# The general path for tokens beyond an expert's slots: 64 unrolled copies become two nested loops on the chip

## The chip, the cores and the metric

The kernel runs on 1 core of one Trainium2 chip, as one launch. The metric is the device time in microseconds (us), the median over several executions. Less is better.

## The reference, cut to what matters

Two layers of a trunk on 256 tokens of width 1024. Each layer mixes tokens (projection, three branches, output projection), normalises, and then sends each token through 2 of 16 experts, chosen by a router whose weights both layers share:

```python
def moe(x2, w_router, router_bias, w1, w3, w2):
    expert_idx, gate_w = route(x2, w_router, router_bias)   # top-1 group of 4, top-2 inside it
    ...
    h = jax.nn.silu(xb @ w1[e]) * (xb @ w3[e])              # per expert: 1024 -> 512
    return h @ w2[e]                                        # 512 -> 1024
    ...
    return jnp.zeros((N + 1, D), x2.dtype).at[slot_tok].add(y)[:N]   # weighted by the gate
```

Everything is float32. An expert can be chosen by any number of tokens, so a kernel with a fixed number of places per expert needs a second path for the tokens that don't fit.

## The kernel before, in words

`body` (line 158) writes out both layers, one after the other, for five engines: TensorE (PE, with PEld for its weight loads), VectorE (DVE), ScalarE (ACT), GpSimd (POOL) and SyncE (SP). The order of each engine's instructions is the order in which the Python code makes them. That order is chosen while the program is built, by a small model of the engines' clocks (`Clock`, line 56): every operation made through the wrapper `Engine` (line 153, so nearly all rows carry L153) advances the model's clock of its engine, and waiting chains of work are put in where the model says that their inputs are ready. The model has no part in the execution.

The experts' part of a layer goes by seven units (`UNITS`, line 28, loop `for j in range(NU)` at line 1413). Six units hold two experts with 64 places each; unit 2 holds four experts with 32 places. The tokens of a unit are gathered into 128 columns (`xg`). For each unit PE does w1 (`hw`, 16 calls on a pair unit, 32 records), some combining of the unit before (`acc`), w3 (`hw` again), a transpose (`ht`) and w2 (`y`). A float32 product is two records per call, a transpose is one. Between these stand, in layer 0, products of the next layer's memory branch (`mk`, `mv`), and for the last two units the transposes that spread the norm's gain and shift (`ln`).

All weights come by DMA, issued on SP in one long stream (`plan` and `pump`; lines 215, 242, 252, 258 and 260 are its issues). A chunk goes into one of 27 slots of on-chip memory as soon as the slot is free, and an issue also waits for a transfer some places earlier to land. For a pair unit, w1, w3 and w2 are four chunks each, and each chunk is two issues (one for each expert), or four for the last. The last unit of a layer takes its w1 and w3 by line 242 and its w2 by lines 258 and 260, in layer 1 the last part of w2 by line 252. PE takes the chunks of w1 and w3 in the order in which they were issued, 8 records for each.

The router step counts the tokens of each expert. `fl` (line 1259) is 1 if a count is over 64 (32 for the four experts of unit 2), else 0. `Go` holds the gates of the tokens that found no place. After unit 5 (`j == NU - 2`, line 1522) `overflow(acc)` is called, once per layer. It is the general path: each engine loads `fl` into a register (line 1288, `TENSOR_LOAD` in the profile) and enters `tc.If(v_ > 0)` (line 1289, `COMPARE_BRANCH`). Inside, the tokens' vectors are transposed (`xo`, 8 times two transposes, 8 copies on DVE), and then all 16 experts times 4 quarters of the hidden width are computed for all 256 tokens, as 64 unrolled copies: 2 DMAs on POOL, 16 products, an activation on ACT, a multiply on DVE, two transposes of a gate column, a multiply on DVE, one more DMA on POOL, and 4 products that add to the accumulators `acc`. SP does nothing inside. Where the branch is not taken, each engine jumps over all that was written for it and then runs an `EVENT_SEMAPHORE` of line 1289 that waits until the engine's own earlier work is done and adds to its semaphore what the path inside would have added. What comes next on an engine stands behind that.

With these inputs the path inside is not taken: no record of `wt`, `xo`, `w2t` or of any other line inside the `If` is in the profile.

In PE's program the `If` stands between the last w2 product of unit 5 and the first w1 product of unit 6. In DVE's and ACT's it stands behind the first half of `scaled` for unit 5 (`yt<-y,gsl`), in SP's behind all issues of which the planner had slots: in layer 1 that is behind the last weight of the kernel.

Of the kernel before, what the change touches and what calls it, by code (L numbers as in the profile page):

```python
# [11 lines left out]
F32 = mybir.dt.float32  # L12
# [4 lines left out]
AF = mybir.ActivationFunctionType  # L17
OP = mybir.AluOpType
# [6 lines left out]
NE = 16  # L25
# [132 lines left out]
def body(tc, out, xT, xtok, memT, pos, cst, par, lay, pw, vb, lnr, wi, wik, wm, wb, wo, w1, w3, w2):  # L158
    nc = tc.nc
    ctx = ExitStack()  # L160
    clk = Clock()
    V, S, G, PE = (Engine(e, k, clk) for e, k in ((nc.vector, "V"), (nc.scalar, "A"), (nc.gpsimd, "G"), (nc.tensor, "P")))
# [4 lines left out]
    sm = ctx.enter_context(tc.tile_pool(name="sm", bufs=2))  # L167
# [8 lines left out]
    def tr(name):  # L176
        return clk.alloc("tr", 2, ps.tile([128, 512], F32, name=name, tag="tr", bufs=2))
# [25 lines left out]
    def again(slot, name, shape, dt=F32):  # L203
        return slots.tile(shape, dt, name=name, tag=held[slot])
# [23 lines left out]
    def get(*key):  # L228
        return live[key]
# [78 lines left out]
    ident = C[:, C_ID:C_ID + 128]  # L308
# [15 lines left out]
    def ln_col(l, w, k):  # L324
        o = P_LN + (l * 4 + w) * 8 + k
        return P[:, o:o + 1]
# [283 lines left out]
    key, shape, src = stream[0]  # L610
# [60 lines left out]
    for l in range(NL):  # L671
# [316 lines left out]
        if l == 0:  # L988
            for k in range(NL):
                o = P_BC + k * NB + B_G  # L990
# [152 lines left out]
        def rt(shape, name, dt=F32, tag=None):  # L1143
            return sm.tile(shape, dt, name=name, tag=tag or "r_" + name, bufs=1)
# [59 lines left out]
        Go = rt([128, 2, 16], "Go")  # L1204
# [82 lines left out]
        def overflow(acc):  # L1287
            v_ = nc.values_load(fl[0:1, 0:1], min_val=0, max_val=1)
            with tc.If(v_ > 0):
                xo = again("nh_h", "xo", [128, 8, 256])  # L1290
                for k in range(8):
                    p = tr("oxt")
                    for i in range(2):
                        PE.transpose(p[:, i * 128:(i + 1) * 128], xt[:, i, k * 128:(k + 1) * 128], ident)
                    if k < 4:
                        V.tensor_copy(xo[:, k], p[:, 0:256])
                    else:
                        V.tensor_scalar(xo[:, k], p[:, 0:256], ln_col(l, 0, k), ln_col(l, 1, k), op0=OP.mult, op1=OP.add)
                for e in range(NE):
                    for f in range(4):  # L1300
                        wt = again("nh_l", "wt", [128, 2, 8, 128])
                        fs = slice(f * 128, (f + 1) * 128)
                        for i, w in enumerate((w1, w3)):
                            nc.gpsimd.dma_start(wt[:, i], w[l, e].rearrange("p (k c) -> p k c", c=512)[:, :, fs])
                        ph = [tr("oh1"), tr("oh3")]
                        for w in range(2):
                            for k in range(8):
                                PE.matmul(ph[w][:, 0:256], wt[:, w, k], xo[:, k], start=k == 0, stop=k == 7)
                        w2t = again("nh_l", "w2t", [128, 1280])
                        ht = w2t[:, 1024:1280]  # L1310
                        S.activation(ht, ph[0][:, 0:256], AF.Silu)
                        V.tensor_tensor(ht, ht, ph[1][:, 0:256], op=OP.mult)
                        for i in range(2):
                            PE.transpose(ph[0][:, 256 + i * 128:384 + i * 128], Go[:, i, e:e + 1].broadcast_to([128, 128]), ident)
                        V.tensor_tensor(ht, ht, ph[0][:, 256:512], op=OP.mult)
                        nc.gpsimd.dma_start(w2t[:, 0:1024], w2[l, e, :, 1024 * f:1024 * f + 1024])
                        for i in range(2):
                            for hf in range(2):
                                PE.matmul(acc[i][hf], ht[:, i * 128:(i + 1) * 128], w2t[:, hf * 512:(hf + 1) * 512],
                                          start=False, stop=False)  # L1320


        acc = []
# [89 lines left out]
        for j in range(NU):  # L1413
# [20 lines left out]
            for nm in ("w1", "w3"):  # L1434
                early_mem(j, nm)
                p = tr("h" + nm)
                for q in range(4):
                    for kk in range(2):
                        k = 2 * q + kk
                        for a in range(len(ex)):  # L1440
                            o = jj * 128 + a * w_
# [50 lines left out]
            p = tr("ht")  # L1492
# [13 lines left out]
            if j < NU - 1:  # L1506
                yp = [pj("y"), pj("y")]
                for f in range(4):
                    for hf in range(2):
                        for a in range(len(ex)):  # L1510
                            PE.matmul(yp[hf][a * w_:(a + 1) * w_], hT[:, f, a * w_:(a + 1) * w_],
                                      get(l, "w2", j, f * len(ex) // 2 + a // 2)[:, a % 2, 0, hf * 512:(hf + 1) * 512],
                                      start=f == 0, stop=f == 3)
                    for b in range(len(ex) // 2):
                        if j == NU - 3 and f == 3:
                            done_as("xt", l, "w2", j, f)
                        else:
                            done(l, "w2", j, f * len(ex) // 2 + b)
                scaled(j, yt, yp[0], 0, 512)
                prev = (j, yp[1])  # L1520
                if j == NU - 2:
                    overflow(acc)
                    ring(NH if l + 1 == NL else RJ[2])
                    if l + 1 == NL:
                        held["gb"] = held.pop("nh_h")
                    else:
                        free("nh_h")
                    free("nh_l")
                if "gb" in held:
                    assert nxt[0] == len(stream)  # L1530
                    gb = load_gb(l, 2, again("gb", "gb", [128, 2, D]))
                continue

            pieces = [(0, 512), (512, 768)] + ([(768, 896), (896, 1024)] if tail else [(768, 1024)])
            for n, (lo_, hi_) in enumerate(pieces):
                p = (tr if n >= 2 else pj)("y")[:, 0:hi_ - lo_]
                for f in range(4):
                    q = f // 2 if n == 0 else min(n, 2) + 1
                    for a in range(2):
                        w = get(l, "w2", j, q)  # L1540
                        if n == 0:
                            w = w[:, 4 * a + 2 * (f % 2):4 * a + 2 * (f % 2) + 2].rearrange("p k c -> p (k c)")
                        elif hi_ - lo_ == 128:
                            w = w[:, 4 * (n - 2) + 2 * a + f // 2, 128 * (f % 2):128 * (f % 2) + 128]
                        else:
                            w = w[:, 4 * a + f]
# [197 lines left out]
```

## Time and profile before

| | us |
|---|---|
| median of 3 runs | 984.54 (983.82 to 985.46) |
| the profiled execution, its own time | 985.81 |
| its span, first to last instruction | 984.0 |
| PE busy | 928.5 (94% of the span) |
| DVE, ACT, POOL busy | 509.3, 372.8, 32.9 |
| data moved by DMA | 292.14 MB, mean 297 GB/s |
| TensorE clock granted, mean | 0.982 of full speed |

Times in the rows are microseconds from the span's start, in the timeline the start and the length of a group of instructions, its engine, line, operation, tiles and shapes, count, and in brackets the idle time before it and what ended that. A name ending in q (PEldq, DVEq) is an engine's sequencer: its register, branch and semaphore instructions, which don't count as busy time. [...]

### The profile page before, as it was taken

To read this page: it belongs to the slowest core of one execution; us is meant where nothing else is said; L and a number is where in the kernel's file an instruction comes from. 1 tells how busy PE (TensorE), PEld (TensorE's weight loads), DVE (VectorE), ACT (ScalarE), POOL (GpSimd) and SP (SyncE) were. 2 spreads that over 40 slices of the span, in tenths; PEclk is the share of its full clock that TensorE was granted. 3 is DMA by queue.
4 is the path that set the end of the run, shared out by engine and by line. 5 is a ranking of instruction groups with operands and counts; after the bars stand their busy time and mean duration, and the time that the engine had idled before them with its cause. 6 is when DMAs were issued, how large, how long until landed. Compare 5 with 4: busy or idle time off the path is not lost.

```text
span 984.0 us, 16526 instructions
## 1 busy us (share of the span) xinstructions
PE 928.5 (94%) x6450; PEld 681.3 (69%) x6450; DVE 509.3 (52%) x1042; ACT 372.8 (38%) x642; POOL 32.9 (3%) x29
## 2 busy tenths in 40 slices
PE   6999999989999999997998999999899899999974
PEld 6999999989954343433488999999899443434422
DVE  5879774559451111142388888854685412111226
ACT  5645667555241010121155644675552210101001
POOL 0000000000010000020022000000000000000101
PEclk9999999999999999998999999999999999999988
DMA  9933263309999999999995213265199999999994
GB/s 345 424 147 125 87 257 129 130 23 417 420 420 365 419 418 419 420 419 417 412 394 197 104 47 118 98 270 201 59 419 420 326 369 419 419 419 419 418 410 138
DMA packets 74461, 292.14 MB, mean 297 GB/s; under 512 B 7168, under 2 KB 13312, under 8 KB 64128
## 3 DMA queue, kind: packets, MB, share of 16 engines
q1 hardware_dynamic: 74368, 290.94, 74.5%
q8 instruction: 54, 0.88, 0.3%
q14 instruction: 39, 0.32, 0.1%
HBM read 289.86 MB, written 1.05 MB: 296 GB/s over the span
## 4 chain that ended last, share of the span: by engine, by line
PE 34%; issue 30%; DMA 26%; DVE 3%; POOL 2%; ACT 1%; SPq 0%; POOLq 0%; DVEq 0%; another core or an unknown queue 0%
DMA ck_w<-w 26%; PE g L153 7%; PE hw L153 5%; PE wb L153 4%; PE wo L153 2%; PE y L153 2%; PE gx L153 2%; PE mv L153 1%; POOL xt L153 1%; PE q L153 1%; PE k L153 1%; PE mq L153 1%; PE u L153 1%; PE v L153 1%; DVE xt L153 1%
## 5 line engine op out<-in xcount | busy, mean ns | idle before, releaser
L153 PE MATMUL hw<-ck_w,xg 128*64 128x512 f32 (+1 forms) x1024 | 218.3, 609 | 15.1 <-DMA ck_w<-w 8.6
L153 PEld LDWEIGHTS hw<-ck_w,xg 128*64 128x64 f32 (+1 forms) x1024 | 66.0, 132 | 146.8 <-issue 111.5
L153 PE MATMUL g<-x_h,wsp 128*128 128x256 f32 x768 | 146.6, 287 | 0.0
L153 PEld LDWEIGHTS g<-x_h,wsp 128*128 128x128 f32 x768 | 121.8, 191 | 1.5 <-issue 0.7
L153 PE MATMUL g<-x_l,wsp 128*128 128x256 f32 x384 | 108.6, 283 | 0.0
L153 DVE SCALAR_TENSOR_TENSOR yt<-y,gsl,yt 128x512 fp32r<-128x512 f32 (+1 forms) x29 | 21.0, 723 | 160.4 <-ACT yt L153 160.4
L153 PE MATMUL y<-ck_w,hs 128*64 128x512 f32 (+3 forms) x560 | 101.1, 559 | 1.1 <-ACT hs L153 0.9
L153 DVE TENSOR_TENSOR wsp<-ck_g,wsp 128x1024 fp32r<-128x1024 f32 x48 | 58.7, 1224 | 43.8 <-ACT wsp L153 43.5
L153 PEld LDWEIGHTS y<-ck_w,hs 128*64 128x64 f32 (+1 forms) x560 | 34.1, 130 | 58.7 <-issue 49.0
L153 PEld LDWEIGHTS g<-x_l,wsp 128*128 128x128 f32 x384 | 73.6, 192 | 0.2
L153 ACT ACTIVATE yt<-y,gsl 128x512 fp32r<-128x512 f32 (+2 forms) x31 | 20.0, 646 | 97.0 <-PE y L153 93.6
L153 ACT CAST wsp<-ck_g 128x1024 fp32r<-128x1024 f32 x48 | 50.0, 1042 | 0.0
L153 PE MATMUL wo<-wsp,mg 128*128 128x256 f32 x384 | 49.2, 285 | 0.0
L153 ACT COPY hs<-ht 128x256 f32<-128x256 f32 x14 | 5.2, 373 | 112.0 <-PE ht L153 112.0
L153 PEld LDWEIGHTS wo<-wsp,mg 128*128 128x128 f32 x384 | 46.9, 192 | 0.0
L153 ACT ACTIVATE hs<-hw 128x512 f32<-128x512 f32 x14 | 8.4, 599 | 94.9 <-PE hw L153 94.9
L153 DVE TENSOR_TENSOR hs<-hs,hw 128x512 f32<-128x512 f32 x14 | 9.6, 688 | 64.7 <-PE hw L153 64.7
L153 DVE TENSOR_TENSOR wsp<-ck_wb,wsp 128x1024 fp32r<-128x1024 f32 x24 | 29.4, 1223 | 19.8 <-ACT wsp L153 19.8
L153 ACT ACTIVATE g<-g,P 128x256 f32<-128x256 f32 x48 | 22.7, 473 | 41.0 <-PE g L153 40.7
L153 PE MATMUL iq<-x_h,wsp 128*128 128x256 f32 x128 | 28.7, 322 | 7.5 <-ACT wsp L153 7.5
L153 ACT CAST wsp<-ck_wb 128x1024 fp32r<-128x1024 f32 x24 | 25.1, 1045 | 22.1 <-PE wb L153 21.6
L153 ACT ACTIVATE xg<-gx,P 128x256 f32<-128x256 f32 (+1 forms) x40 | 20.8, 522 | 25.7 <-PE gx L153 25.3
(281 smaller groups left out, 1795.0 us busy)
## 6 DMA issues: line engine op xcount, KB each, us to landing
ck_w<-w SPq DMA_DIRECT2D x286, 512.0 KB, 10.0
ck_w<-w SPq DMA_DIRECT2D x48, 1024.0 KB, 17.7
ck_g<-wi SPq DMA_DIRECT2D x24, 1024.0 KB, 4.9
ck_wb<-wb SPq DMA_DIRECT2D x12, 1024.0 KB, 4.8
ck_wo<-wo SPq DMA_DIRECT2D x8, 1024.0 KB, 6.1
ck_mk<-wm SPq DMA_DIRECT2D x4, 1024.0 KB, 10.5
ck_mv<-wm SPq DMA_DIRECT2D x4, 1024.0 KB, 11.4
ck_q<-wi SPq DMA_DIRECT2D x4, 1024.0 KB, 16.6
```

The source lines that it names most:

```text
L153: return f(*args, **kw)
```

## The change

The two Python loops over experts and quarters inside the `If` become two nested loops on the chip (`tc.For_i`). What is inside is written once. The slices of the weights are addressed by the loop registers, and the gate column is first copied to a small tile `ge`, from which the transposes read. The `If`, its condition and its place stay, and nothing outside it is touched.

```diff
-                for e in range(NE):
-                    for f in range(4):
-                        wt = again("nh_l", "wt", [128, 2, 8, 128])
-                        fs = slice(f * 128, (f + 1) * 128)
-                        for i, w in enumerate((w1, w3)):
-                            nc.gpsimd.dma_start(wt[:, i], w[l, e].rearrange("p (k c) -> p k c", c=512)[:, :, fs])
...
-                        V.tensor_tensor(ht, ht, ph[1][:, 0:256], op=OP.mult)
-                        for i in range(2):
-                            PE.transpose(ph[0][:, 256 + i * 128:384 + i * 128], Go[:, i, e:e + 1].broadcast_to([128, 128]), ident)
-                        V.tensor_tensor(ht, ht, ph[0][:, 256:512], op=OP.mult)
-                        nc.gpsimd.dma_start(w2t[:, 0:1024], w2[l, e, :, 1024 * f:1024 * f + 1024])
...
+                with tc.For_i(0, NE) as e, tc.For_i(0, 4) as f:
+                    wt = again("nh_l", "wt", [128, 2, 8, 128])
+                    for i, w in enumerate((w1, w3)):
+                        src = w[l].rearrange("e p (k f c) -> e p k f c", f=4, c=128)[bass.ds(e, 1), :, :, bass.ds(f, 1)]
+                        nc.gpsimd.dma_start(wt[:, i], src.rearrange("e p k f c -> p (e k) (f c)"))
...
+                    V.tensor_tensor(ht, ht, ph[1][:, 0:256], op=OP.mult)
+                    ge = sm.tile([128, 2], F32, name="ge", tag="ve")
+                    V.tensor_copy(ge, Go[:, :, bass.ds(e, 1)].rearrange("p i o -> p (i o)"))
+                    for i in range(2):
+                        PE.transpose(ph[0][:, 256 + i * 128:384 + i * 128], ge[:, i:i + 1].broadcast_to([128, 128]), ident)
+                    V.tensor_tensor(ht, ht, ph[0][:, 256:512], op=OP.mult)
+                    src = w2[l].rearrange("e p (f c) -> e p f c", f=4)[bass.ds(e, 1), :, bass.ds(f, 1)]
+                    nc.gpsimd.dma_start(w2t[:, 0:1024], src.rearrange("e p f c -> p (e f c)"))
```

The lines left out are the same on both sides but for their indentation: the two products with `xo`, the activation, and the four products into `acc`.

## Rows read from the trace of the kernel before

**Rows 1.** The page: busy us and instructions; then busy tenths of DMA in 40 slices.

```profile
PE 928.5 (94%) x6450; PEld 681.3 (69%) x6450; DVE 509.3 (52%) x1042; ACT 372.8 (38%) x642; POOL 32.9 (3%) x29
...
DMA  9933263309999999999995213265199999999994
```

**Rows 2.** Instructions of line 1289, both layers: duration ns min/median/max, first and last start.

```profile
L1289 PEldq COMPARE_BRANCH  x2: 5808/5880/5952, 453.5 to 933.8; - x2
L1289 ACTq COMPARE_BRANCH  x2: 45/45/45, 457.1 to 934.9; - x2
L1289 DVEq COMPARE_BRANCH  x2: 68/70/72, 458.0 to 935.7; - x2
L1289 PEldq EVENT_SEMAPHORE  x2: 51/51/51, 459.4 to 939.9; - x2
L1289 ACTq EVENT_SEMAPHORE  x2: 17/17/17, 462.1 to 935.4; - x2
L1289 SPq COMPARE_BRANCH  x2: 45/49/53, 462.2 to 962.0; - x2
L1289 DVEq EVENT_SEMAPHORE  x2: 21/21/21, 463.4 to 941.1; - x2
```

**Rows 3.** Timeline of PE behind the branch of layer 0, and the last w2 part.

```profile
463.67 5.00 PE L153 MATMUL hw<-ck_w,xg 128*64 128x512 f32 x16 [6.33 <-DMA ck_w<-w]
...
493.39 1.95 PE L153 MATMUL y<-ck_w,hs 128*64 128x256 f32 x16
```

**Rows 4.** Timeline of PE in layer 1: first, last w3 chunk, end.

```profile
941.36 8.52 PE L153 MATMUL hw<-ck_w,xg 128*64 128x512 f32 x32 [6.03 <-DVEq L1289]
...
957.55 1.94 PE L153 MATMUL hw<-ck_w,xg 128*64 128x512 f32 x8
...
970.67 1.25 PE L153 MATMUL cb<-yt,Pq 128*128 128x128 f32 x8
```

**Rows 5.** Timeline of DVE: its last operation ahead of each branch.

```profile
457.32 0.75 DVE L153 SCALAR_TENSOR_TENSOR yt<-y,gsl,yt 128x512 fp32r<-128x512 f32 x1 [5.68 <-ACT yt L153]
...
935.28 0.75 DVE L153 SCALAR_TENSOR_TENSOR yt<-y,gsl,yt 128x512 fp32r<-128x512 f32 x1 [6.37 <-ACT yt L153]
```

**Rows 6.** Instruction fetches: the page's DMA kinds, whole span (packets, MB, share).

```profile
q8 instruction: 54, 0.88, 0.3%
```

**Rows 7.** DMA kinds in the stretch 933 to 946 us, around layer 1's branch.

```profile
q8 instruction: 2, 0.03, 0.9%
q14 instruction: 3, 0.02, 0.4%
```

**Rows 8.** Windows: us, busy times (instructions) of PE, PEld, DVE, ACT, POOL, PEclk, DMA share, GB/s.

```profile
463.70:470.20 6.50, 6.50 (x29) 3.09 (x30) 2.23 (x2) 0.45 (x1) 0.00 (x0) 0.79 1.03 416
935.30:941.40 6.10, 0.07 (x3) 0.07 (x3) 0.73 (x1) 0.00 (x0) 0.00 (x0) 0.68 1.03 413
941.40:947.90 6.50, 6.50 (x24) 2.29 (x26) 0.00 (x0) 0.00 (x0) 0.00 (x0) 0.78 1.03 415
820.00:900.00 80.00, 79.36 (x469) 32.78 (x466) 13.25 (x28) 11.00 (x19) 0.00 (x0) 1.00 1.03 419
```

**Rows 9.** Issues of w1's first chunk in layer 0, unit 6 (line 242).

```profile
L242 SPq DMA_DIRECT2D ck_w<-w x2: 338/338/338, 443.3 to 444.4; - x2
...
DMA to landing us min/median/max: 11.8/11.8/11.8
```

**Rows 10.** The last issue of w2 in layer 0 (line 260).

```profile
L260 SPq DMA_DIRECT2D ck_w<-w x1: 1130/1130/1130, 476.0 to 476.0; - x1
...
DMA to landing us min/median/max: 8.7/8.7/8.7
```

**Rows 11.** The last issue of w3 in layer 1 (line 242).

```profile
L242 SPq DMA_DIRECT2D ck_w<-w x1: 674/674/674, 943.7 to 943.7; - x1
...
DMA to landing us min/median/max: 10.8/10.8/10.8
```

**Rows 12.** Issues of w2's first two chunks in layer 1 (line 258), behind the branch's fetches.

```profile
DMA to landing us min/median/max: 9.8/9.9/10.0
```

More of the change, by code (lines that the diff above doesn't have):

```diff
@@ L1298, in overflow @@
                         V.tensor_scalar(xo[:, k], p[:, 0:256], ln_col(l, 0, k), ln_col(l, 1, k), op0=OP.mult, op1=OP.add)
-                for e in range(NE):
-                    for f in range(4):
-                        wt = again("nh_l", "wt", [128, 2, 8, 128])
-                        fs = slice(f * 128, (f + 1) * 128)
-                        for i, w in enumerate((w1, w3)):
-                            nc.gpsimd.dma_start(wt[:, i], w[l, e].rearrange("p (k c) -> p k c", c=512)[:, :, fs])
[L1305 to L1311, printed above, removed]
-                        V.tensor_tensor(ht, ht, ph[1][:, 0:256], op=OP.mult)
-                        for i in range(2):
-                            PE.transpose(ph[0][:, 256 + i * 128:384 + i * 128], Go[:, i, e:e + 1].broadcast_to([128, 128]), ident)
-                        V.tensor_tensor(ht, ht, ph[0][:, 256:512], op=OP.mult)
-                        nc.gpsimd.dma_start(w2t[:, 0:1024], w2[l, e, :, 1024 * f:1024 * f + 1024])
[L1317 to L1320, printed above, removed]
@@ new lines, in overflow @@
+                with tc.For_i(0, NE) as e, tc.For_i(0, 4) as f:
[3 more added lines that the diff above has]
+                        nc.gpsimd.dma_start(wt[:, i], src.rearrange("e p k f c -> p (e k) (f c)"))
+                    ph = [tr("oh1"), tr("oh3")]
+                    for w in range(2):
+                        for k in range(8):
+                            PE.matmul(ph[w][:, 0:256], wt[:, w, k], xo[:, k], start=k == 0, stop=k == 7)
+                    w2t = again("nh_l", "w2t", [128, 1280])
+                    ht = w2t[:, 1024:1280]
+                    S.activation(ht, ph[0][:, 0:256], AF.Silu)
+                    V.tensor_tensor(ht, ht, ph[1][:, 0:256], op=OP.mult)
[6 more added lines that the diff above has]
+                    nc.gpsimd.dma_start(w2t[:, 0:1024], src.rearrange("e p f c -> p (e f c)"))
+                    for i in range(2):
+                        for hf in range(2):
+                            PE.matmul(acc[i][hf], ht[:, i * 128:(i + 1) * 128], w2t[:, hf * 512:(hf + 1) * 512],
+                                      start=False, stop=False)
```

## The prediction, made before the change was run

> **What bounds the kernel now.** I first read the page's slices: the DMA engines are full from the tenth slice to the twenty-first and again from the thirtieth to the last but one, stretches that take in the experts' stages of both layers [rows 1]. There the weights set the pace. Then I looked for the changed lines. Nothing inside the `If` left a record, so with these inputs the path is skipped in both layers, and all the change can move is what it costs to skip it. The view of line 1289 shows that cost [rows 2]. PE's branch takes 5.81 and 5.95 us by itself, at 453.5 and 933.8. DVE's takes 0.07, but its next instruction comes 5.4 us after it both times (458.0 to 463.4, 935.7 to 941.1). ACT loses 5 us in layer 0 (457.1 to 462.1), nothing in layer 1 (934.9 to 935.4). SP, with nothing inside, passes in 0.05.
>
> PE's timeline shows what comes of it: idle 6.33 and then 6.03 us [rows 3, 4]. PE starts again 0.27 us after DVE's late instruction both times (463.4 to 463.67; 941.1 to 941.36), and in layer 1 the trace names it. In layer 0 it names a DMA. I don't follow it there: the first product behind the branch needs the first chunk of w1, issued at 443.3 and 444.4 and landed 11.8 us later, by 456.2 [rows 9]. So PE waits for DVE, and DVE for its own jump.
>
> What is in the jump? The skipped code of DVE is 8 copies and 64 times 2 operations, 136 and the waits. That of PE is 16 transposes, and 64 times 16 + 4 products and 2 transposes. At four instructions for a product (two records, each with a weight load) and two for a transpose that is 32 + 64 x 84, some 5,400. The trace's fetches say how far that is: PE and PEld executed 12,900 instructions [rows 1] in a run with 54 packets on queue 8 [rows 6], 239 for each, so PE jumps over some 22 packets' worth. And around the branch of layer 1 the fetch queues moved two packets for PE and three for the others in 13 us [rows 7], where 54 in 984 us would be 0.7 for PE. I read the 5 to 6 us as waiting for code that had not been fetched, behind a full DMA system.
>
> **The change part by part.** *Copies removed.* Inside are left 8 + 3 operations on DVE, one on ACT, and on PE 32 + 84 = 116 instructions, with the loops' own control some 150: 0.6 of a packet. The skip then ends in code that is being fetched ahead anyway. That a short skip is free is shown by ACT in layer 1 (64 activations, 0.4 us) and by SP. That ACT's same skip cost 5 us in layer 0 says that it depends on where the code lies, and bounds the claim: per branch the cost is between 0.05 and 5.95 us. I take 0.2, since the skip is now much shorter than ACT's.
>
> [...]
>
> *Layer 0.* DVE's last operation ends at 457.32 + 0.75 = 458.07 [rows 5]; with 0.2 for the branch and 0.27 for the handover PE starts at 458.5 instead of 463.67: 5.2 us. Then the clock: PE runs at 0.79 of full speed for 6.5 us behind the stall [rows 8], 1.4 us of work lost, which an idle of about 1 us should not bring about (bounds 0 and 1.4). So 5.2 to 6.6. Do the weights allow it? The last issue of w2 lands at 476.0 + 8.7 = 484.7 [rows 10], and PE uses it at 493.39 [rows 3]: room for 8.7. The earlier chunks have as much or more, so it isn't taken back there. What is late next is PE itself, and behind it the start of layer 1, which takes its input from these products; there DMA is half idle [rows 1], so the shift is handed on until the weights of layer 1 start, that many us earlier. I take 6.5.
>
> *Layer 1.* PE could start at 935.28 + 0.75 + 0.47 = 936.5, 4.9 earlier, with the same 1.4 of clock. But here PE has little to gain on: the last of w3 lands at 943.7 + 10.8 = 954.5 [rows 11], and PE begins those products at 957.55 [rows 4]. 3.05 us is all, unless the weights come earlier. They might: issues land after 10.8 us here, and after 9.9 just behind [rows 12], so the fetches may hold the stream up by 0.9; by the moved bytes (413 and 415 against 419 GB/s [rows 8]) it is 0.15. So 3.2 to 4.0; I take 3.5. The weights are late next.
>
> *Added work.* The copy to `ge`, the address arithmetic and the loops' control are inside and not run: 0, whatever they cost. *Left as it is:* the five loads of the flag. *Order.* The planner's clock now goes through the body once instead of 64 times. What it decides afterwards depends on differences between engines; after one pass as after 64, PE is last and ACT first, so I expect the same order: 0, with 1.5 us either way if some chain moves. POOL's skip is long done when POOL is next needed: 0, and SP's costs 0.05 now.
>
> **Sum.** 6.5 + 3.5 = 10.0. The profiled execution took 985.81 in all (span 984.0 and 1.8 around it), so it would take 975.8; it lies 1.27 above the median of 984.54, which makes 974.5. With the bounds 8.4 and 10.6, and 1.5 for the order: 972.4 to 977.6.
>
> **The rivals.**
>
> *Half of it.* One jump in one layer still misses, or the DMA that the trace names in layer 0 was the true end of that wait. Then one term is left: 984.5 - 6.5 = 978.0, or 984.5 - 3.5 = 981.0. For it: ACT, with one miss and one hit on the same code. Against: 11 DVE operations are a twelfth of 136.
>
> *The distance isn't it.* DVE's 5.4 us would be something that every taken branch of DVE has here, and PE's 5.9 would hide behind it. Then nothing moves: 984.5. For it: DVE skips only 136 operations, far less than PE, and yet waits as long. Against: ACT's 0.4 us in layer 1, and the three packets on queue 14 in [rows 7]. [...]
>
> [...]
>
> **How the numbers follow.** Both stalls go: 0.62. Half: 0.13. No change: 0.08. Barrier: 0.17. The likeliest is 974.5. A measurement of this kernel can tell about 0.2%, 2 us. The range leaves out the barrier and reaches over the half case to the no-change case, and down by the 1.5 of the order and some 2 us for the layer border, where DVE and POOL share a stretch that may fall together differently: 970.5 to 984.5. Faster is the first two and a little of the third: 0.76; same 0.07; slower 0.17.
>
> **What would show it.** Right: line 1289 on PE and DVE under 0.5 us, PE idle about 1 us at either branch, the granted clock full behind it, the weights' DMA full as before, and layer 1 starting some 6 us earlier. In layer 1 PE should now wait for single chunks of w3. Wrong: DVE's next instruction still 5 us behind its branch; PE waiting on another engine's line 1289 until SP arrives; new semaphore or drain instructions on the way around; or layer 0 gaining and the start of layer 1 not.

## The result, and the profile after

The changed kernel takes 979.27 us, median of 4 runs (978.02 to 979.70), beside 984.99 us for the kernel before (4 runs, 983.82 to 985.46; one more than stood in its table). The ratio is 0.9935 [0.9916, 0.9954] (in brackets the 95% interval): faster by 5.7 us, 0.6%, where the forecast of 974.5 said 10. The profiled execution took 979.70, its span is 978.0; both are 6.0 to 6.1 under those of the kernel before.

The page of the changed kernel comes first: busy us and instructions of PE, then the busy tenths of DMA in 40 slices and the instruction fetches (packets, MB, share).

```profile
PE 927.9 (95%) x6450; PEld 680.7 (70%) x6450; DVE 510.2 (52%) x1042; ACT 372.7 (38%) x642; POOL 32.7 (3%) x29
...
DMA  9943263309999999999996213266199999999995
...
q8 instruction: 52, 0.85, 0.3%
q14 instruction: 31, 0.25, 0.1%
```

Each engine executes as many operations as before [rows 1]. Two fetch packets fewer arrive on queue 8 (54 before, [rows 6]). The full stretches of DMA stand where they stood. (By these rows a packet of queue 8 is 16 KB and one of queue 14 is 8 KB. That PE's code comes on queue 8 and DVE's and ACT's on queue 14 is inferred from the packets' times, in the table under runs 4, 9 and 12.)

The view of line 1289 of the changed kernel answers to [rows 2].

```profile
L1289 PEldq COMPARE_BRANCH  x2: 318/336/353, 454.1 to 931.5; - x2
L1289 ACTq COMPARE_BRANCH  x2: 45/48/50, 457.8 to 932.9; - x2
L1289 ACTq EVENT_SEMAPHORE  x2: 17/17/17, 457.9 to 933.0; - x2
...
L1289 DVEq COMPARE_BRANCH  x2: 56/64/72, 458.6 to 933.3; - x2
L1289 DVEq EVENT_SEMAPHORE  x2: 21/21/21, 458.8 to 933.7; - x2
L1289 SPq COMPARE_BRANCH  x2: 45/49/53, 462.8 to 958.6; - x2
```

PE's branch costs 0.3 us instead of 5.9. DVE's event comes 0.2 to 0.4 us behind its branch instead of 5.4. ACT loses nothing in either layer (0.2 us). SP still comes last and nobody waits for it. POOL's jump, for which nobody waits, ends 0.2 to 0.5 us behind its branch instead of 5.1. So the jumps are cheap on every engine, and no barrier took their place: PE restarts at 459.07 and 934.00, SP passes at 462.8 and 958.6.

What PE made of it is in its timeline (only groups behind an idle time, and the three that answer to [rows 3, 4]), with its waits at the layer border in the kernel before below.

```profile
459.07 3.65 PE L153 MATMUL hw<-ck_w,xg 128*64 128x512 f32 x16 [1.12 <-DVEq L1289]
...
487.45 1.95 PE L153 MATMUL y<-ck_w,hs 128*64 128x256 f32 x16
...
524.54 0.45 PE L153 MATMUL ikw<-x_h,wsp 128*72 128x256 f32 x2 [3.21 <-DVE wsp L153]
531.19 0.39 PE L153 MATMUL q<-x_h,wsp 128*128 128x256 f32 x1 [2.31 <-ACT iqs L153]
...
934.00 6.88 PE L153 MATMUL hw<-ck_w,xg 128*64 128x512 f32 x26 [1.01 <-DVEq L1289]
...
951.02 1.95 PE L153 MATMUL hw<-ck_w,xg 128*64 128x512 f32 x8
...
964.66 1.25 PE L153 MATMUL cb<-yt,Pq 128*128 128x128 f32 x8
```

```profile
517.48 0.39 PE L153 MATMUL iq<-x_l,wsp 128*128 128x256 f32 x1 [0.42 <-DVE x_l L153]
...
520.25 0.39 PE L153 MATMUL iq<-x_l,wsp 128*128 128x256 f32 x1 [1.79 <-DVE x_l L153]
...
535.11 0.39 PE L153 MATMUL q<-x_h,wsp 128*128 128x256 f32 x1 [1.05 <-ACT iqs L153]
```

Read as a walk along the program, each start against its partner before:

| place | before | after | ahead of before |
|---|---|---|---|
| PE's branch, layer 0 [rows 2] | 453.5 | 454.1 | -0.6 |
| last w2 part, layer 0 [rows 3] | 493.39 | 487.45 | 5.94 |
| PE's branch, layer 1 [rows 2] | 933.8 | 931.5 | 2.3 |
| last w3 chunk, layer 1 [rows 4] | 957.55 | 951.02 | 6.53 |
| last products [rows 4] | 970.67 | 964.66 | 6.01 |

Layer 0 gained 0.6 + 5.94 = 6.5 us, layer 1 gained 6.01 - 2.3 = 3.7. These are the two terms of the forecast, 6.5 and 3.5. The 0.6 us by which the changed kernel was behind came near 400 us, ahead of the first branch; between the traces of the runs below this difference goes from 2.0 behind to 1.9 ahead, so I don't count it as the change's.

But of the 5.94 us only 2.3 were left at the second branch. I matched the two traces product by product (PE executes them in the same order but for one exchanged pair near 875 us) and call the time by which a product starts earlier the lead. It is still 5.93 in `iq` of layer 1 (516 us before), grows to 10.15 near the end of `iq`, is 3.92 when `q` begins and 2.42 some 2.5 us later; then it stays between 2.1 and 2.7 up to layer 1's branch. So 3.3 us were lost within 30 us, at the layer border, where PE now waits for `wsp` (a chunk of weights, split in two parts for the products) and `iqs` (524.54 and 531.19 above).

The windows of the changed kernel show the clock (us, busy times of PE, PEld, DVE, ACT, POOL, PEclk, DMA share, GB/s; PEclk is the mean of the TensorE clock granted, 1.00 at full speed, DMA share the busy share of the 16 DMA engines).

```profile
458.00:464.00 6.00, 4.93 (x27) 2.61 (x28) 3.05 (x3) 1.99 (x2) 0.00 (x0) 1.00 1.03 417
...
524.00:530.00 6.00, 4.34 (x22) 4.09 (x22) 5.79 (x12) 0.42 (x1) 0.00 (x0) 0.72 0.53 178
530.00:536.00 6.00, 4.81 (x27) 4.81 (x28) 3.69 (x5) 5.59 (x8) 0.00 (x0) 0.72 0.98 374
...
936.00:942.00 6.00, 5.71 (x23) 1.88 (x22) 0.00 (x0) 0.00 (x0) 0.00 (x0) 1.00 1.03 417
```

At the border of the kernel before:

```profile
518.00:524.00 6.00, 4.21 (x24) 4.01 (x24) 6.00 (x3) 1.19 (x3) 4.36 (x2) 0.75 0.45 150
```

Behind both branches the granted clock is now full, where it was 0.79 and 0.78 [rows 8]. At the border it fell in the kernel before too, in this one stretch (0.96 in the next, full behind that); now it is 0.72 in two, with the waits for `wsp` and `iqs`.

What held `wsp` is in DVE's timeline of the changed kernel, with POOL's beside it: four operations of one gain-and-shift step (`next_x`, `xt<-xt,gb`).

```profile
511.19 10.64 POOL L153 TENSOR_TENSOR xt<-xt,gb 128x1024 f32<-128x1024 f32 x4 [15.15 <-DMA gb<-lnr]
...
512.11 2.50 DVE L153 CAST aux<-aux 128x256 f32<-128x256 int32 x1
514.64 2.46 DVE L153 TENSOR_SCALAR aux<-aux,rc 128x256 f32<-128x256 f32 x1
517.13 4.85 DVE L153 TENSOR_SCALAR aux<-aux 128x256 f32<-128x256 f32 x2
```

In the kernel before the same stretch reads so:

```profile
511.64 10.79 POOL L153 TENSOR_TENSOR xt<-xt,gb 128x1024 f32<-128x1024 f32 x4 [9.67 <-PE xtr L153]
...
512.25 2.35 DVE L153 TENSOR_TENSOR x_l<-xraw,x_h 128x512 fp32r<-128x512 f32 x1
514.53 0.53 DVE L153 TENSOR_SCALAR xraw<-xtr,P 128x256 f32<-128x256 f32 x1
514.99 5.21 DVE L153 TENSOR_TENSOR x_l<-xraw,x_h 128x512 fp32r<-128x512 f32 x2
520.12 4.53 DVE L153 TENSOR_TENSOR wsp<-ck_iq,wsp 128x1024 fp32r<-128x1024 f32 x2
524.57 0.28 DVE L153 CAST aux<-aux 128x256 f32<-128x256 int32 x1
524.89 0.35 DVE L153 TENSOR_SCALAR aux<-aux,rc 128x256 f32<-128x256 f32 x1
```

This is the main reading. POOL's stretch stayed at 511 to 522 us, because it now starts when the row `gb` (gain and shift) has landed: issued at 495.3, that transfer takes 15.7 us behind a full weight stream (DMA share 1.00 to 1.01 from 495 to 511 us), and POOL waits 15.15 us for it. Before, the row was issued at 494.7 and landed after 16.8 us, at 511.5, as the transposes `xtr` ended for which POOL waited there. All the rest moved 6 us ahead beneath it. Before, POOL's four operations stood beside four of DVE: three on `x_l` and the first of the two splits of `iq` (3.40 us; the second, behind POOL's end, takes the usual 1.23). Now they stand beside four operations on `aux` (the rotary angles, called rope below), each of which takes 2.4 to 2.5 us instead of 0.28 to 0.35. The split of `ikw`, for which PE waits, comes behind them. The second wait comes through ACT: its `iqs<-iq` at 530.68 stands behind its two operations on `aux` (529.24 and 530.36), and these wait for the rope (9.58 and 0.70 us). The operations hit before are short again (`x_l` 0.69 to 0.74 us, the split 1.23), which is the growth to 10.15; the loss behind it is larger.

In layer 1 the weights capped the gain as forecast. The changed kernel's last issue of w3 (line 242, answering to [rows 11]):

```profile
L242 SPq DMA_DIRECT2D ck_w<-w x1: 333/333/333, 941.0 to 941.0; - x1
...
DMA to landing us min/median/max: 10.0/10.0/10.0
```

It lands at 951.0 and PE begins on it at 951.02. The 3.05 us of room that it had before are used up to the last tenth.

### The profile page after: what moved, and what is told of

Same layout as the page of the kernel before. It is cut to its first block, busy times and chain, and to the rows that moved or that the text cites. A ratio compares the mean times of both kernels' runs of the same rounds, so it can differ in the third digit from the quotient of the medians.

```text
span 978.0 us, 16510 instructions
## 1 busy us (share of the span) xinstructions
PE 927.9 (95%) x6450; PEld 680.7 (70%) x6450; DVE 510.2 (52%) x1042; ACT 372.7 (38%) x642; POOL 32.7 (3%) x29
## 3 DMA queue, kind: packets, MB, share of 16 engines
HBM read 289.86 MB, written 1.05 MB: 297 GB/s over the span
## 4 chain that ended last, share of the span: by engine, by line
issue 30%; DMA 13%; PE 7%; DVE 2%; POOL 2%; ACT 0%; POOLq 0%; SPq 0%; DVEq 0%; another core or an unknown queue 0%
DMA ck_w<-w 11%; PE hw L153 3%; DMA gb<-lnr 2%; PE y L153 1%; POOL xt L153 1%; PE gx L153 1%; DVE xt L153 1%; PE mk L153 0%; PE acc L153 0%; POOL yn L153 0%; DVE val L153 0%; DVE st L153 0%; DVE wsp L153 0%; PE ln L153 0%; DVE hs L153 0%
## 5 line engine op out<-in xcount | busy, mean ns | idle before, releaser
L153 PE MATMUL iq<-x_h,wsp 128*128 128x256 f32 x128 | 25.3, 298 | 8.6 <-ACT wsp L153 8.6
```

Source lines behind the costliest of these rows:

```text
L153: return f(*args, **kw)
```

## The experiments

Each ratio is to the kernel before on the same chip, as its median went from 983.91 to 988.22 between chips.

**The layer border: runs 1 and 2.** `pass` in place of the four POOL operations, in the kernel before (run 1) and the changed one (run 2). Both leave out the gain and shift of layer 0's last norm on the residual.

```diff
-                        G.tensor_tensor(xt[:, i], xt[:, i], gb[:, o], op=op)
+                        pass
```

> The kernel before, without GpSimd's four operations that apply gain and shift to layer 0's output (the residual of layer 1 is then left unscaled). Theory A, GpSimd's four operations hold up VectorE at the border of the layers: the products iq run without their 2.2 us of waits and without the stretch at half clock, the time falls by 3 to 4 us, to about 981. Rival B, the border is set by weights and GpSimd is harmless: 985, no change.

> The changed kernel without the same four operations. Theory A: the 6.5 us that PE gains behind the branch of layer 0 now reach layer 1 whole, so the distance to the kernel before without them is 6.5 + 3.9 = 10.4 us, and the time is about 971. Rival B: what was lost at the border stays lost, 979, and the distance stays under 6.

Measured: run 1 979.79, ratio 0.9946 [0.9929, 0.9964]; run 2 968.80, ratio 0.9833 [0.9802, 0.9864]. The four operations cost either kernel time, 4 us before and some 10 after. Without them the change is worth 11.0 us (10.4 were expected), and layer 0's term arrives whole at the second branch: the lead of run 2's trace over run 1's is -1.0 ahead of the first branch, 5.8 behind it, 5.8 behind the border and 6.4 ahead of the second branch. So the loss at the border is these operations' doing.

**Which engine's jump: run 3.** The kernel before, with DVE's two multiplies written in the first of the 64 copies only (the other 63, on the path that isn't taken, are left out).

```diff
-                        V.tensor_tensor(ht, ht, ph[1][:, 0:256], op=OP.mult)
+                        if (e, f) == (0, 0):
+                            V.tensor_tensor(ht, ht, ph[1][:, 0:256], op=OP.mult)
...
-                        V.tensor_tensor(ht, ht, ph[0][:, 256:512], op=OP.mult)
+                        if (e, f) == (0, 0):
+                            V.tensor_tensor(ht, ht, ph[0][:, 256:512], op=OP.mult)
```

> The kernel before with its 64 copies, but VectorE's two multiplies only in the first (in the path that is not taken, so the output is unchanged). PE still skips some 5,400 instructions, VectorE 10 operations. Theory A, PE mostly waits for VectorE's jump: in layer 0 PE restarts when its own branch ends, near 459.7 instead of 463.7 (most of the gain), in layer 1 near 940.1 instead of 941.4 (little of it): about 981. Rival B, PE's own far jump is what costs: 985 as before.

Measured: 984.57, ratio 0.9994 [0.9976, 1.0012]. Line 1289 in this run, and PE's two restarts:

```profile
L1289 PEldq COMPARE_BRANCH  x2: 5805/5868/5932, 451.6 to 932.9; - x2
L1289 ACTq COMPARE_BRANCH  x2: 45/45/45, 455.3 to 934.0; - x2
L1289 DVEq COMPARE_BRANCH  x2: 56/64/72, 456.1 to 934.8; - x2
L1289 DVEq EVENT_SEMAPHORE  x2: 21/21/21, 456.3 to 935.3; - x2
L1289 PEldq EVENT_SEMAPHORE  x2: 51/51/51, 457.5 to 938.9; - x2
...
L1289 ACTq EVENT_SEMAPHORE  x2: 17/17/17, 460.3 to 934.5; - x2
...
460.39 1.97 PE L153 MATMUL hw<-ck_w,xg 128*64 128x512 f32 x4 [4.93 <-ACTq L1289]
...
939.25 3.59 PE L153 MATMUL hw<-ck_w,xg 128*64 128x512 f32 x8 [4.85 <-PEq L1289]
```

DVE's gap is gone (0.2 and 0.5 us), and the kernel's time is as before; the forecast's theory A fell, its rival held. PE restarts only 1.4 and 1.2 us sooner behind its branch. In layer 0 it waits for ACT's jump (455.3 to 460.3), in layer 1 for its own (932.9 to 938.9). So DVE's jump alone does not make the stall: three jumps run side by side, and the last to end decides.

**How long a jump may be: runs 4, 9 and 12.** The changed kernel, with bare one-element copies for DVE inside the path that is skipped, 126 in run 4, 1000 in run 9, 320 in run 12.

```diff
+                for _ in range(126):
+                    nc.vector.tensor_copy(xo[:, 0, 0:1], xo[:, 0, 1:2])
```

> The changed kernel with 126 small copies on VectorE put into the skipped path ahead of the loops, so that VectorE skips about as much as before and PE and ScalarE as little as after. Theory A: VectorE's next instruction is again 5 us late in both layers, PE waits for it, and the time is back at 984 to 985. Rival B, PE's far jump was the cost: 979, as after. Rival C, a jump of about 136 instructions is still covered by what is fetched ahead: 979 and VectorE's gap under 0.5 us.

> The changed kernel with 1000 copies of one element written for DVE inside the path that is skipped, ahead of the loops; 136 of them were jumped over in 0.6 us. Theory A: what counts is how much code lies under the jump, on DVE as on PE. Then a jump over 1000 instructions misses in both layers: DVE's event of line 1289 comes 4 to 6 us after its branch, PE waits for it, and the time is that of the kernel before or up to 4 us under it (ratio 0.996 to 1.002). Rival: the length of DVE's jump does not matter by itself, and the kernel before paid for something else that its multiplies bring (their waits on other engines). Then DVE's event still comes 0.5 us behind the branch and the time stays that of the changed kernel, ratio 0.9915 to 0.9955.

> The changed kernel with 320 copies of one element written for DVE inside the path that is skipped. 136 were jumped over in 0.6 us, 1000 in 5.5 us. The kernel before had 136 operations there, and waited 5.4 us; its 64 pairs of multiplies carry three and two waits on other engines, and if each wait beyond the first is an instruction of its own that makes 136 + 64 x (2 + 1) = 328 instructions. Theory A: the length in instructions decides, waits counted. Then 320 bare copies miss as the kernel before did: DVE's event of line 1289 comes 5 to 6 us behind its branch in both layers, and the ratio is 0.996 to 1.004. Rival: the jump of the kernel before was late for another reason than its length (between 136 and 1000 instructions lies a border beyond 320). Then the event comes 0.4 to 0.6 us behind the branch and the ratio is that of the changed kernel, 0.9915 to 0.9955.

Measured: 126 copies 978.98, ratio 0.9936 [0.9915, 0.9956], as the changed kernel (rival C; theory A fell). 1000 copies 988.46, ratio 1.0031 [1.0015, 1.0046], a little over its forecast; its trace loses 1.3 us more at the layer border than the kernel before. 320 copies 987.88, ratio 1.0016 [1.0001, 1.0031]. DVE's rows of line 1289 in run 4:

```profile
L1289 DVEq COMPARE_BRANCH  x2: 63/68/72, 456.9 to 929.9; - x2
L1289 DVEq EVENT_SEMAPHORE  x2: 21/21/21, 457.5 to 930.4; - x2
```

and in run 12:

```profile
L1289 DVEq COMPARE_BRANCH  x2: 68/70/72, 456.6 to 933.9; - x2
...
L1289 DVEq EVENT_SEMAPHORE  x2: 21/21/21, 462.0 to 939.2; - x2
...
939.52 5.91 PE L153 MATMUL hw<-ck_w,xg 128*64 128x512 f32 x18 [6.00 <-DVEq L1289]
```

DVE's event comes 0.5 to 0.6 us behind its branch in run 4, 5.3 and 5.4 in run 12, and 5.4 and 5.5 in run 9. So the price is a step, not a slope: next to nothing for 137 operations, the full price at some 330, and no more at a thousand. The jump of DVE alone gives back the whole gain of the change, although PE's and ACT's are short in run 12 (0.3 and 0.2 us). The kernel before skipped 136 operations on DVE and paid, where 137 bare ones are free. Its multiplies carry waits on other engines, which by the count that went on record with run 12 would make 328 instructions, if each wait beyond the first is one of its own. That agrees with 320 bare ones missing, but it is the author's estimate: no trace shows how the waits are laid down.

What a late engine waits for can be read from the times of the fetch packets in the same traces. Ahead of each late instruction one packet of instruction fetch ends, and the engine goes on 1.2 to 1.5 us later:

| jump | branch | packet | goes on |
|---|---|---|---|
| PE, before, layer 0 | 453.49 | 456.93 to 457.87 | 459.30 |
| ACT, before, layer 0 | 457.14 | 460.55 to 460.86 | 462.08 |
| DVE, before, layer 0 | 457.96 | 461.57 to 461.88 | 463.39 |
| DVE, run 12, layer 0 | 456.59 | 460.12 to 460.43 | 461.96 |
| DVE, run 9, layer 0 | 458.15 | 461.77 to 462.08 | 463.62 |

Each packet starts 3.4 to 3.6 us behind the branch. In the changed kernel and in run 4 no packet falls between DVE's branch and its next instruction, in either layer. And where no long jump is, packets come while PE works on: from 820 to 900 us of the kernel before it is busy for 79.36 us of the 80 [rows 8], and four packets of queue 8 start in that time (829.72, 847.85, 870.28, 899.50). So the prediction's reading, that a late engine waits for code not yet fetched, agrees with the packets; that each carries just the code that its engine needs is inferred from the times.

**The loops themselves: run 5.** The kernel before with one copy and no loop, which leaves out 63 of the 64 parts of a path that isn't taken.

```diff
-                for e in range(NE):
-                    for f in range(4):
+                for e in range(1):
+                    for f in range(1):
```

> The kernel before with one copy in the skipped path instead of 64 and no loop (15 experts and 3 quarters are left out of a path that is not taken; the output is unchanged). Theory A, only the length of the skipped code matters: as the changed kernel, 978 to 980, each branch under 0.5 us. Rival B, the loops add something to the way around: the one copy is 2 us or more faster than the changed kernel, under 977.

Measured: 977.63, between its two forecasts, ratio 0.9899 [0.9862, 0.9936], whose interval overlaps that of the changed kernel. The times alone can't tell the two apart; the traces can. The branches cost 0.2 to 0.4 us on PE and 0.3 to 0.6 on DVE. PE's lead over the kernel before grows by 6.7 us over the first branch and by 5.2 over the second, in the changed kernel by 6.6 and 5.2. It then goes from 6.72 to 3.43 us at the border, with the rope operations at 2.49, 2.45 and 4.84 us. So the loops add 0.2 us at most on the way around; what counts is that the skipped code is short.

**Moving the collision: runs 6, 7 and 8.** The changed kernel; in run 6 the row `gb` is loaded earlier, so that POOL need not wait for it; in run 7 the four operations are given to DVE, behind the products of `k`; in run 8 the load is held back until the rope operations are planned.

```diff
+                gbx = load_gb(l, 2, take("gb", [128, 2, D])) if l + 1 < NL else None
...
-            def next_x(l=l, y7=y7):
+            def next_x(l=l, y7=y7, gb=gbx):
...
-                gb = load_gb(l, 2, take("gb", [128, 2, D]))
```

```diff
+                yield flag("k")
...
-                        G.tensor_tensor(xt[:, i], xt[:, i], gb[:, o], op=op)
+                        V.tensor_tensor(xt[:, i], xt[:, i], gb[:, o], op=op)
```

```diff
+                yield flag("rope")
                 gb = load_gb(l, 2, take("gb", [128, 2, D]))
```

> The changed kernel with the transfer of gain and shift (gb) issued ahead of the next layer's weights, so that GpSimd can start its four operations when the tokens' vectors are ready and not when that transfer lands. Theory A, the gain of layer 0 was lost because GpSimd's stretch stood still at 511 us while the rest moved 6 us ahead, and met the rope operations of VectorE: with it moved along, the shift is handed on whole, 975 to 976. Rival B, the loss has another cause: 979.

> The changed kernel with GpSimd's four operations made on VectorE instead, planned behind the projection of k. Theory A: the border is free as without them (969), VectorE pays 4 times 1.2 us where it has room: 969 to 974, faster than both kernels. Rival B, VectorE is the bound there and the 4.9 us show in full, with the planner's other order on top: 977 or more.

> The changed kernel with the transfer of gain and shift issued only behind the rope tables, so that GpSimd's stretch of 10.6 us comes later, beside other operations of VectorE. Theory A: the rope operations run at 0.3 to 0.6 us again, the loss at this place is gone: 971 to 976. Rival B, the stretch holds up the next chain of VectorE as much: 978 to 980.

Measured: run 6 974.23, ratio 0.9879 [0.9846, 0.9912]; run 7 975.75, 0.9886 [0.9855, 0.9918]; run 8 969.25, 0.9817 [0.9781, 0.9852]. In run 6 POOL starts at 503.45 and hits the same operations as in the kernel before (`x_l` 2.35 and 5.21 us). The lead behind layer 0 is 8.09 us in its trace (1.5 of it from ahead of the branch) and still 8.07 at the products of `mq` in layer 1: with POOL moved along, the shift is handed on whole. That is the same proof as runs 1 and 2, with nothing left out. Run 7 comes out between its two forecasts. It has no POOL operation there, keeps 10.24 us up to 591 us, and loses 6 of them by 717 us: the planner now chose another order of PE's products from 580 us on, and PE waits 7.12 us for ACT's `pp` up to 685.78, where the kernel before waits 2.52. Why that chain is late was not tried. Run 8 is the best of all, beyond its forecast: POOL and DVE's rows in its trace are

```profile
523.52 11.92 POOL L153 TENSOR_TENSOR xt<-xt,gb 128x1024 f32<-128x1024 f32 x4 [26.80 <-DMA gb<-lnr]
...
524.70 5.66 DVE L153 TENSOR_TENSOR wsp<-ck_q,wsp 128x1024 fp32r<-128x1024 f32 x2 [1.52 <-ACT wsp L153]
530.39 2.79 DVE L153 COPY iqs<-iqs 32x1024 f32<-32x1024 f32 x1
533.21 4.45 DVE L153 TENSOR_TENSOR wsp<-ck_k,wsp 128x1024 fp32r<-128x1024 f32 x2
```

POOL still holds up four operations of DVE (three of the four splits shown, and the copy of `iqs`), but PE does not stand still for any of them between 506 and 560 us.

**Does the late row help by itself? Runs 10 and 11.** Run 8's edit on the kernel before, and run 8 once more on the same chip.

> The kernel before, 64 copies and all, with the load of the row of gain and shift held back until the rope operations are planned, as in the run that moved it late in the changed kernel. Theory A: the four POOL operations cost time by the DVE operations that they hold up, in either kernel, and the jumps over the copies cost theirs independently. Then this kernel still stalls 5 to 6 us at both branches, DVE's x_l operations take 0.7 and 1.5 us, and the gain is about that of the kernel before without the POOL operations: 977 to 981 beside 984.5, ratio 0.9925 to 0.9965. The distance to the changed kernel with the same edit (run here too) is 9 to 11 us, so the loops' whole gain shows. Rival: the late place owes its gain to where the loops put the border, and at before's border the POOL operations hit the operations of q and k just as hard: 983 to 986, ratio 0.998 to 1.002, with the split operations behind 520 us at twice their time.

> The changed kernel with the row of gain and shift held back until the rope operations are planned, once more, on the chip of the run beside it. If the first result holds on another chip: ratio 0.979 to 0.985, 9 to 11 us under the kernel before with the same edit. If that result came from that chip alone, the ratio is that of the changed kernel, 0.9915 to 0.9955.

Measured: run 10 986.06, ratio 1.0009 [0.9989, 1.0029]; run 11 968.35, ratio 0.9836 [0.9814, 0.9859]. Run 11 repeats run 8. Run 10's forecast was wrong and its rival right: the same edit that saves the changed kernel some 10 us (from a ratio of 0.9935 to 0.9817 and 0.9836) saves the kernel before nothing. Its trace says why.

```profile
525.07 10.03 POOL L153 TENSOR_TENSOR xt<-xt,gb 128x1024 f32<-128x1024 f32 x4 [24.37 <-DMA gb<-lnr]
...
525.50 4.92 DVE L153 TENSOR_SCALAR aux<-aux 128x256 f32<-128x256 f32 x2
530.45 2.44 DVE L153 SCALAR_TENSOR_TENSOR aux<-aux 128x256 f32<-128x256 f32 x1
532.93 2.31 DVE L153 TENSOR_SCALAR aux<-aux 128x256 f32<-128x256 f32 x1
...
536.11 0.58 PE L153 MATMUL q<-x_h,wsp 128*128 128x256 f32 x1 [7.54 <-ACT iqs L153]
```

In run 8 the last rope operations begin at 521.52 and are done before POOL starts at 523.52. Here they begin at 525.50, just under POOL's late stretch. ACT's operation on `aux` waits for the last of them, its `iqs<-iq` stands right behind that (535.60), and PE, which needs that, is idle for 7.54 us. The 4.2 us that the free `x_l` brings are lost again, and 4 more. So the late place isn't good in itself. It is good for the order of time that the shorter skip brings, and the two edits together are worth more than their sum.

## Why the prediction was right or wrong

*What bounds the branches: right in kind, incomplete in one part.* The skipped code's length makes the stall, as runs 5, 9 and 12 show, and the fetch packets agree with the reason given. The prediction followed only DVE ("PE waits for DVE, and DVE for its own jump"). Run 3 shows that PE's and ACT's jumps stood right behind it. The forecast was saved by the change shortening all of them at once.

*Layer 0, the stall and the clock: right.* 6.5 us were forecast and 6.5 measured at the last w2 part; the granted clock is full (1.00) behind idle times of 1.12 us there and 1.01 us in layer 1, and the weights held nothing up.

*"so the shift is handed on until the weights of layer 1 start": this step failed.* That DMA is half idle there was taken as proof that nothing at the border keeps its place. One thing did: the row `gb`, for whose landing POOL waits. POOL's 10.6 us then fell on other DVE operations, which lie just ahead of a split for which PE waits. Of 5.94 us of lead 2.3 reached the second branch; in runs 2 and 6 the lead reached it whole. So its own sign, "layer 1 starting some 6 us earlier", did not come. The bounds had named the pair, "where DVE and POOL share a stretch that may fall together differently", at 2 us; it was 3.3: PE's idle times there went from 0.42 + 1.79 + 1.05 to 3.21 + 2.31 us, 2.3 more, and the same products took 1.1 us longer, at the granted clock of 0.72. The 979.27 lies beyond what the sum's own bounds allowed (972.4 to 977.6), and within the stated range only because that reached up to the half case and the no-change case. That is the range's width, not the mechanism.

Beside POOL the operations on `aux`, `x_l` and `wsp` take 2.3 to 3.4 us each, one for each of POOL's operations (2.4 to 3.4 us), and each ends 0.1 to 1.1 us behind POOL's, the later the longer it takes by itself (`aux` 0.15, `x_l` 0.55, `wsp` 1.09 behind; 0.28 to 0.35, 0.69 and 1.23 by themselves). `xraw<-xtr,P` in the kernel before, whose input PE had just written, keeps its 0.53 us. What makes the one wait for the other was not shown.

*Layer 1: right.* 3.5 forecast, 3.7 measured. Room of 3.05 us was used up exactly. The last w3 lands 3.5 us earlier than before, of which 2.3 is the kernel's lead at the branch, so the stream gained 1.2 (forecast 0.15 to 0.9).

*Added work and order: right.* The loops cost 0.2 us at most (run 5), and PE's order of products is the same but for one pair.

*The rivals.* No jump is left ("half of it"), and the DMA that the trace had named in layer 0 was not the true end of that wait: PE now restarts at 459.07, behind DVE. "The distance isn't it" fell with runs 9 and 12, and its counter-evidence, a short DVE skip that waits, is solved in kind: 137 bare operations are free and 331 are not. The barrier (chance 0.17), in which all engines would meet at the `If` and PE would wait for SP, did not come: SP passes at 958.6 and PE restarts at 934.00. Neither the loops nor the copies are run here, so no run shows what a turn of the loops costs or does with the semaphores.

*Left open:* why ACT's jump of the kernel before missed in layer 0 and not in layer 1 (the same in runs 3 and 10, so it is no accident of one execution); where between 137 and 331 operations the step lies. Runs 1, 2, 6, 7, 8 and 11 gain another 1.6 to 1.7 us between 717 and 808 us, where the granted clock in the window 750 to 770 us is 1.00 in them, as it is in run 9, which gains 1.3 us there and is no faster in all, and 0.91 to 0.97 in all others. So part of what runs 1, 2, 6, 7, 8 and 11 saved does not come from the border, and whether their edits keep the clock up there or executions of one kernel differ in it was not tried.

## What to carry to other kernels

Code that is skipped had a price here, and it was a step (on DVE 0.5 to 0.6 us for 137 operations, 5.3 to 5.5 for 331 and for some 1010): keep the body of a branch that is seldom taken short on every engine at once, because one long jump alone, DVE's in run 12, restored the whole stall. A gain early in a kernel is handed on only if everything behind it moves along; look for whatever a fixed event (a transfer behind a full stream) holds in place, and see what slides under it. Two edits that meet at such a place must be timed together: the late row was worth nothing before the change and some 10 us after it.

## What the runs showed of the hardware that was not expected

A jump over 331 or over some 1010 DVE operations cost the same 5.3 to 5.5 us under a full weight stream, one over 137 cost 0.5 to 0.6 us. The late jumps ended 1.2 to 1.5 us behind a packet of instruction fetch. Each POOL operation at the border (2.4 to 3.4 us, f32) held up one DVE operation on `aux`, `x_l`, `wsp` or `iqs` until 0.1 to 1.1 us behind its own end, whatever that operation's size: 0.28 us became 2.50, and 1.23 became 2.3 to 3.4; `xraw<-xtr,P` was not held up (0.53). Four POOL operations hit four of DVE, in the kernel before, the changed one and runs 6, 8 and 10 alike. So the loss is counted in DVE operations hit, and what it costs the kernel depends on who waits for them.
